# Eighteen feed-forward blocks formed by seven products in place of eight

## The chip, the cores and the metric

The kernel runs on one core of a Trainium2 chip. The metric is the time of one execution on the device, in microseconds (us); the kernel before takes 2004.53 us, the median of three runs (2004.17 to 2005.12). Five engines run their own queues of instructions side by side: PE (TensorE, the matrix products), DVE (VectorE), ACT (ScalarE), POOL (GpSimd) and SP (SyncE, which here only issues transfers). They exchange data through the on-chip memory SBUF and the accumulator banks PSUM, and wait for each other by semaphores.

## The reference, cut to what matters

The program is a stack of two blocks: first two layers of mixers at width 1024, then a block with a mixer and a feed-forward part. The change concerns the feed-forward part, whose mathematics is

```
def conv_gated_mlp(xn, w_up_gate, conv_w_ffn, w_down):
    u, g = jnp.split(xn @ w_up_gate, 2, axis=-1)
    u = causal_dwconv_2(u, conv_w_ffn)          # three taps over the positions
    return (jax.nn.gelu(u) * g) @ w_down

ffn = conv_gated_mlp(rms_norm(h, g_pre_ffn), w_up_gate, conv_w_ffn, w_down)
h = h + rms_norm(ffn, g_post_ffn)
```

with 512 tokens behind 16 meta tokens, D = 1024, 2 x 2816 columns of `w_up_gate`, all float32. The kernel forms 516 of the 528 positions here: four meta tokens are enough for the taps.

## The kernel before

Activations lie transposed, channels on the 128 partitions and positions along the free axis, as eight tiles for the 1024 channels (the K tiles). A float32 value is carried as the sum of a high and a low part in a format that PE multiplies at full rate, so one float32 product is three PE products: high by high, low by high, high by low (`mm3`, lines L101 to L103 of the trace). A `split` makes the parts: a cast on ACT gives the high part (L77), a subtraction on DVE gives the low part (L78); `split_scaled` (L81 and L82) does the same with the gain of the norm multiplied in.

The feed-forward loop runs over 22 pairs: pair m forms block m of u and block m of g, each 128 columns of `w_up_gate`. For a block, SP loads its weights into `wraw` (128 x 8 x 128, 512 KB, three buffers), ACT and DVE split them into `whi` and `wlo` (128 x 1024, three buffers), and PE forms two halves of 258 positions (the g block leaves out the meta tokens: 254 and 258), each 8 K tiles x 3 products. A pair is so 96 products on PE. The norm's factor per position, `rb` (tile `rbc` in the trace), is not in the activations yet: DVE multiplies it in as it empties the PSUM bank (L1274 into `u`, L1284 into `act`). Then come the taps (a tensor_scalar at L1276 and two scalar_tensor_tensor at L1278, all DVE, 128 x 512), the gelu on ACT (L1280) and the gate, `act * cv`, on POOL (L1285). Pairs 6 to 13 also turn one eighth of the residual `h` round by four PE transposes (L1263) and four DVE copies (L1265). After the 22 pairs the products with `w_down` (`ps_d`) follow, for which `act` is split too, into `xh` and `xl`.

The order of instructions on every engine is set by a scheduler that plans the program with a model of its times; the code gives the order of the data only. Every engine takes its instructions in that fixed order, and an instruction that waits holds up all behind it. Tiles come from pools with a fixed number of buffers, and a new tile waits until the buffer's last reader is done. Six PSUM banks (2 to 7) serve the products of this part, and two serve the transposes and the statistics (`ps_st`, L228) of the norm ahead of it.

Of the kernel before, what the change touches and what calls it, by code (L numbers as in the profile page):

```python
# [34 lines left out]
def kernel(ctx: ExitStack, tc: tile.TileContext, a, out):  # L35
# [355 lines left out]
    def tok_proj(w, c0, xs, raw=None):  # L391
        """256 columns, tokens on partitions: yields (t, psum)."""
# [9 lines left out]
    def tok_pairs(w, c0, xs, fine):  # L402
        """The same with the products of two t in one bank."""
# [12 lines left out]
    # ======================= layer 0 =======================  # L416
    w = a["l0_w_in"]
    with ExitStack() as l0:
# [7 lines left out]
        # what the end of a part uses, on the other side: the next part begins before it is free  # L426
# [13 lines left out]
        def silu_gate(ps):  # L440
            """silu of a z projection"""
# [14 lines left out]
        m_st = lt("m_st", n=(4, 128), dt=BF16)  # [s, t]: -NEG where s > t, for each chunk  # L456
# [6 lines left out]
        # input gates from row 0 on, forget gates from row 32 on  # L463
# [27 lines left out]
        V.tensor_tensor(ig, ig, em, op=ALU.subtract)  # a = i - b  # L491
# [25 lines left out]
        # values by token, a column of ones behind them  # L517
# [22 lines left out]
        def others():  # L540
            """The other parameters, the meta tokens, lambda."""
# [21 lines left out]
            # -(e1 - e2 + lam_init)  # L563
# [11 lines left out]
        for hd_ in range(4):  # L575
# [13 lines left out]
            # scores, keys on partitions  # L589
# [8 lines left out]
            # keys by token, weighted  # L598
# [6 lines left out]
            # states before chunks 1 to 3: [C | n], and the output of every chunk: [numerator | denominator]  # L605
# [28 lines left out]
            # output gate, norm, z gate  # L634
# [37 lines left out]
        for hd_ in range(8):  # L672
            j = hd_ % 2
            # queries [high 0, low 0], [low 1, high 1]; keys [high 0, high 0], [high 1, high 1], [low 0, low 1]
# [14 lines left out]
            # [low 1, low 1], so that products into one bank for both maps use all rows  # L689
# [7 lines left out]
            # the maps transposed, blocks [key block, query block] for key blocks up to the query block  # L697
# [6 lines left out]
            for qb in range(4):  # L704
# [4 lines left out]
                # both maps in one bank where they fit  # L709
# [23 lines left out]
                # e0/l0 - lam e1/l1  # L733
# [49 lines left out]
    # ======================= layer 1 =======================  # L783
# [4 lines left out]
    with ExitStack() as l1:  # L788
# [6 lines left out]
        with tc.tile_pool(name="l1", bufs=1) as lp:  # L795
# [12 lines left out]
            triu = lt("triu", 1, 128)  # 1 where column >= partition  # L808
# [17 lines left out]
                # the high and the low part side by side: products of 256 columns  # L826
# [57 lines left out]
    # ======================= block two: mixer =======================  # L884
    w = a["w_in_2"][0]
    with ExitStack() as b2:
# [23 lines left out]
        # the meta tokens at rows 0 and 32 of every product for their keys (for the two heads of a pair), and again  # L910
        # 64 rows on, where the lower part of their values goes
# [20 lines left out]
        # minus one where the key in the row is not before the key in the column  # L932
# [4 lines left out]
        m_st = mt_("m_st", 1, (2, 128), BF16)  # [s, q], twice: NEG where s >= q  # L937
        m_qm = mt_("m_qm", 1, (2, 4), BF16, MR)  # the same, queries from Q0
# [26 lines left out]
        # values by token: [head 0 | zeros | head 1] for each pair of heads and key block  # L965
# [3 lines left out]
        # keys 2 of the second head above zeros, so that both heads' products into one bank use all rows  # L969
# [4 lines left out]
        def values(g):  # L974
            """Two pairs of heads."""
# [32 lines left out]
        def soft(ps, p=128, n=S):  # L1008
            """log(1 + e^z), as float32 and split; z clamped above, where the factor left is zero in float32."""
# [36 lines left out]
        for m in range(KT):  # L1046
            kt = tt("t1", 2)
            evac_r(proj2(next(kw_), xs, 0, 264), 0, 264, kt)
            # keys [high 0, low 0], [low 1, high 1]; queries twice [high 0, high 0], [high 1, high 1]
# [62 lines left out]
            for hh in range(2):  # L1112
                # keys 1 and 3, then keys 0
# [137 lines left out]
    with ExitStack() as ff:  # L1251
# [6 lines left out]
        def residual(i):  # L1258
# [5 lines left out]
            for t in range(4):  # L1264
                V.tensor_copy(ht[t][:, i * 128:(i + 1) * 128], ps[:, t * 128:(t + 1) * 128])  # L1265
# [87 lines left out]
```

## Time and profile before

| | before |
|---|---|
| median of three runs | 2004.53 us |
| profiled execution, its span | 2002.4 us |
| busy: PE | 1980.3 us (99%) |
| busy: DVE | 1261.7 us (63%) |
| busy: ACT | 964.3 us (48%) |
| busy: POOL | 252.0 us (13%) |
| the feed-forward pairs 0 to 21, about | 1633 to 1883 us |
| the down projection, about | 1883 to 1996 us |

The profile comes from one execution; its span, from the first to the last instruction, is 2.1 us under the median of the runs. The busy time of an engine is the time in which at least one of its instructions ran. PE's products are pipelined, so that one that is shown to take 0.28 us may start 0.12 us behind the one before; what a product costs is therefore read from the time of a stretch over its count, not from its own duration. A row of the timeline gives start, duration, engine, line, operation, what was written from what, the tile's size, how many such instructions are drawn together, and in square brackets how long the engine sat idle ahead of it and what ended that. `L78` is line 78 of the kernel before.

### The profile page before, as it was taken

How to read it: one execution, taken by the hardware profiler on the slowest of the kernel's cores; microseconds unless marked ns; L12 is line 12 of the kernel's file. 1: busy time of each engine (PE TensorE's matmuls, PEld its weight loads, DVE VectorE, ACT ScalarE, POOL GpSimd, SP SyncE). 2: the span in 40 equal slices, each digit the busy share in tenths (PEclk: the TensorE clock that was granted, in tenths of full speed). 3: DMA queues.
4: the chain of work that ended last, by engine and by line, in shares of the span. 5: the costliest groups of instructions: out<-in, count | busy, mean ns of one | idle time of the engine just before them, and what ended most of it. 6: DMA issues, size and time to landing. Idle time of an engine off the chain costs nothing.

```text
span 2002.4 us, 33293 instructions
## 1 busy us (share of the span) xinstructions
PE 1980.3 (99%) x13398; PEld 1805.0 (90%) x13398; DVE 1261.7 (63%) x2143; ACT 964.3 (48%) x1815; POOL 252.0 (13%) x339
## 2 busy tenths in 40 slices
PE   8999999999999999999999999999999999999998
PEld 6999988887899888889999999999999999999886
DVE  6667667668662576664877867677344485565533
ACT  5555566668655643354745544545222452222322
POOL 1011000000030111100521212110001031111000
PEclk9999999999999999999999999999999999999999
DMA  6223332222433333243221222222333533333332
GB/s 175 70 75 88 85 85 65 73 74 75 142 115 105 88 97 87 85 138 117 86 64 44 64 61 61 60 64 64 101 95 95 154 111 101 111 91 95 95 95 74
DMA packets 259768, 181.36 MB, mean 91 GB/s; under 512 B 8866, under 2 KB 244607, under 8 KB 259615
## 3 DMA queue, kind: packets, MB, share of 16 engines
q1 hardware_dynamic: 258303, 178.69, 30.0%
q8 instruction: 105, 1.72, 0.4%
q0 software_dynamic: 256, 0.52, 0.1%
q14 instruction: 48, 0.39, 0.1%
q10 hardware_dynamic: 1056, 0.04, 0.0%
HBM read 168.59 MB, written 10.63 MB: 90 GB/s over the span
## 4 chain that ended last, share of the span: by engine, by line
PE 95%; DVE 3%; ACT 1%; DMA 1%; issue 0%; POOL 0%; DVEq 0%; POOLq 0%; ACTq 0%
PE ps L101 18%; PE ps L103 17%; PE ps L102 17%; PE ps_v L103 5%; PE ps_v L101 5%; PE ps_v L102 5%; PE ps_o L101 3%; PE ps_o L102 3%; PE ps_o L103 3%; PE ps_d L101 2%; PE ps_d L103 2%; PE ps_d L102 2%; PE ps_z L1028 2%; PE ps_o L1108 1%; DVE yo L266 1%; PE ps_z L1081 1%
## 5 line engine op out<-in xcount | busy, mean ns | idle before, releaser
L102 PE MATMUL ps<-xl,whi 128*128 128x258 f32 (+3 forms) x2112 | 654.5, 311 | 3.1 <-DVE xl L82 3.0
L101 PE MATMUL ps<-xh,whi 128*128 128x258 f32 (+3 forms) x2112 | 654.7, 313 | 0.8 <-ACT xh L81 0.6
L103 PE MATMUL ps<-xh,wlo 128*128 128x258 f32 (+3 forms) x2112 | 653.7, 311 | 0.0
L77 ACT CAST whi<-wraw 128x1024 fp32r<-128x1024 f32 (+2 forms) x315 | 314.6, 1004 | 471.5 <-PE ps L102 284.8
L78 DVE TENSOR_TENSOR wlo<-wraw,whi 128x1024 fp32r<-128x1024 f32 (+2 forms) x315 | 390.2, 1243 | 180.6 <-ACT whi L77 178.2
L102 PEld LDWEIGHTS ps<-xl,whi 128*128 128x128 f32 x2112 | 399.1, 189 | 27.9 <-DVE xl L82 4.7
L103 PEld LDWEIGHTS ps<-xh,wlo 128*128 128x128 f32 x2112 | 398.5, 189 | 24.2 <-issue 0.5
L101 PEld LDWEIGHTS ps<-xh,whi 128*128 128x128 f32 x2112 | 396.8, 189 | 25.6 <-ACT xh L81 1.5
L101 PE MATMUL ps_v<-whi,xh 128*128 128x256 f32 x896 | 254.2, 285 | 4.5 <-ACT xh L81 4.1
L103 PE MATMUL ps_v<-whi,xl 128*128 128x256 f32 x896 | 253.4, 285 | 1.4 <-DVE xl L82 1.3
L102 PE MATMUL ps_v<-wlo,xh 128*128 128x256 f32 x896 | 254.2, 285 | 0.0
L101 PEld LDWEIGHTS ps_v<-whi,xh 128*128 128x128 f32 x896 | 169.4, 189 | 7.4 <-ACT xh L81 5.6
L103 PEld LDWEIGHTS ps_v<-whi,xl 128*128 128x128 f32 x896 | 169.8, 190 | 3.2 <-DVE xl L82 2.4
L102 PEld LDWEIGHTS ps_v<-wlo,xh 128*128 128x128 f32 x896 | 170.3, 190 | 1.5 <-issue 0.2
L103 PE MATMUL ps<-hi,wlo 128*128 128x258 f32 x384 | 108.6, 283 | 0.0
L101 PE MATMUL ps<-hi,whi 128*128 128x258 f32 x384 | 107.7, 282 | 0.0
L895 DVE TENSOR_TENSOR t<-ps,rbc 128x258 f32<-128x258 f32 (+1 forms) x96 | 40.3, 424 | 64.1 <-PE ps L103 63.5
L102 PE MATMUL ps_o<-xl,whi 128*128 128x512 f32 x192 | 75.6, 394 | 0.0
L101 PE MATMUL ps_o<-xh,whi 128*128 128x512 f32 x192 | 75.4, 395 | 0.0
L103 PE MATMUL ps_o<-xh,wlo 128*128 128x512 f32 x192 | 74.5, 394 | 0.0
L103 PEld LDWEIGHTS ps<-hi,wlo 128*128 128x128 f32 x384 | 72.6, 189 | 0.0
L101 PEld LDWEIGHTS ps<-hi,whi 128*128 128x128 f32 x384 | 72.4, 189 | 0.0
(536 smaller groups left out, 3443.6 us busy)
## 6 DMA issues: line engine op xcount, KB each, us to landing
wraw<-in_l_w_in_dram SPq DMA_DIRECT2D x112, 512.0 KB
wraw<-in_w_in_dram SPq DMA_DIRECT2D x64, 512.0 KB
wraw<-in_w_up_gate_dram SPq DMA_DIRECT2D x44, 512.0 KB
wraw<-in_l_w_out_dram SPq DMA_DIRECT2D x24, 512.0 KB
wraw<-in_w_down_dram SPq DMA_DIRECT2D x22, 512.0 KB
wraw<-in_l_w_out_dram SPq DMA_DIRECT2D x16, 256.0 KB
wraw<-in_w_proj_attn_dram SPq DMA_DIRECT2D x8, 512.0 KB
wraw<-in_w_proj_conv_dram SPq DMA_DIRECT2D x8, 512.0 KB
```

The lines of the kernel that those rows point to most:

```text
L77: A.copy(hi, src)
L78: V.tensor_tensor(lo, src, hi.bitcast(F32), op=ALU.subtract)
L101: T.matmul(ps, lhsT=ah, rhs=bh, start=first, stop=False, **kw)
L102: T.matmul(ps, lhsT=ah, rhs=bl, start=False, stop=False, **kw)
L103: T.matmul(ps, lhsT=al, rhs=bh, start=False, stop=last, **kw)
L266: mult = (G if i % 4 == 3 else V).tensor_tensor(yo[i][:, c], yo[i][:, c], r[:, c], op=ALU.mult)
L895: V.tensor_tensor(dst[:, i * hn:(i + 1) * hn], ps, rb[:, c0 + i * hn:c0 + (i + 1) * hn], op=ALU.mult)
L1028: T.matmul(ps, lhsT=m_, rhs=x_[:, c0:c0 + n], start=False, stop=False, **kw)
L1081: T.matmul(ps, lhsT=k2[hh][r, ks], rhs=ql[r, qs], start=False, stop=False, **kw)
L1108: T.matmul(po[:, n0:], lhsT=l_[:, b, hh:hh + 2, :].rearrange("p a d -> p (a d)"), rhs=a_[r_][:, c0:c0 + S - n0], start=po_first[0], stop=F ...
```

## The change

The sum over K is cut into its two halves (K tiles 0 to 3 and 4 to 7), the positions into their two halves of 258, and the pair of blocks u and g is taken together: u and g, at both halves of the positions, are the four blocks of a product of two 2 x 2 block matrices. Such a product needs eight block products in the plain way. Strassen's identity, in the form of Winograd, needs seven, with sums and differences of blocks ahead of them and behind them. The change uses it for pairs 4 to 21; pairs 0 to 3 stay as they were.

- **Weights.** `seven_w` forms four sums of 128 x 512 on POOL, in the tiles `sa` and `sb`, and splits 3.5 tiles of 128 x 1024 (`r1`, `sa`, `sb`, half of `r2`) in place of two.
- **Activations.** The identity adds positions of one half to those of the other, so the norm's factor has to be in the activations first. Beside pairs 0 to 3, `xn` is formed from `h`, the gain and `rb` (DVE, 128 x 516, eight times), then `seven_x` forms four differences of 128 x 258 on POOL for each of four couples of K tiles, and splits 258, 516 and 1032 columns of each.
- **Products.** Seven products of 4 K tiles x 3 x 258 columns make 84 instructions on PE per pair. ACT copies four results from PSUM to SBUF (`keep`, tile `sn`), DVE adds a PSUM bank and such a copy three times (`o11`, `o12`, `o21`, in place of the four multiplications by `rb`), POOL adds two copies once (`o22`).
- **Around it.** `h` gets a pool of its own, `ht` and `hl` use buffers of the pool `xs`, the last gain is loaded after the pairs. The eight spatial weights of layer 1 are loaded by SP's queue, no longer by POOL's.

```diff
@@ helpers beside mm3 and proj @@
+    HK = KT // 2
+
+    def add(o, x_, y_, op=ALU.add, eng=None):
+        return (eng or G).tensor_tensor(o, x_, y_, op=op)
+
+    def seven_w(pool, r1, r2):
+        sa = pool.tile([128, KT, 128], F32, tag="sa", name="sa", bufs=4)
+        sb = pool.tile([128, KT, 128], F32, tag="sa", name="sb", bufs=4)
+        lo, hi = slice(0, HK), slice(HK, KT)
+        add(sb[:, lo], r2[:, lo], r2[:, hi])
+        add(sa[:, lo], sb[:, lo], r1[:, lo], ALU.subtract)
+        add(sa[:, hi], r1[:, lo], r2[:, lo], ALU.subtract)
+        add(sb[:, hi], r1[:, hi], sa[:, lo], ALU.subtract)
+        w = {}
+        for raw, names in ((r1, "12"), (sa, "67"), (sb, "53"), (r2[:, hi], "4")):
+            sp_ = split_w(raw)
+            ...
+        return w
+
+    def seven_x(pool, tmp, p, xa, xb, n, out):
+        tq = tmp.tile([128, 4, n], F32, tag="tq", name="tq")
+        h0, h1 = slice(0, n), slice(n, 2 * n)
+        t1, t2, t3, t4 = (tq[:, i] for i in range(4))
+        add(t1, xa[:, h1], xa[:, h0], ALU.subtract)
+        add(t3, xb[:, h1], xa[:, h1], ALU.subtract)
+        add(t2, xb[:, h1], t1, ALU.subtract)
+        add(t4, xb[:, h0], t2, ALU.subtract)
+        for src, names in ((xa[:, h0], "1"), (xb, "23"), (tq.rearrange("p a b -> p (a b)"), "5674")):
+            sp_ = [pool.tile([128, n * len(names)], F32R, tag=f"sx{names}{r}{p}", name=f"sx{r}") for r in "hl"]
+            split(src, *sp_)
+            ...
+
+    def seven(sw, sx, n, snp, o11, o12, o21, o22):
+        def product(nm, b, start):
+            if start:
+                bank[b] = pst("mm", n, f"ps_s{b}")
+            wh, wl = sw[nm]
+            for k in range(HK):
+                mm3(bank[b], wh[:, k], wl[:, k], *sx[nm, k], start and k == 0, k == HK - 1, **kw)
+            return bank[b]
+
+        def keep(ps):
+            t_ = snp.tile([128, n], F32, tag="sn", name="sn", bufs=5)
+            A.copy(t_, ps)
+            return t_
+
+        s1 = keep(product("1", "x", True))
+        add(o11, product("2", "y", True), s1, eng=V)
+        u2 = keep(product("6", "x", False))
+        s7 = keep(product("7", "w", True))
+        u4 = keep(product("5", "x", False))
+        add(o12, product("3", "z", True), u4, eng=V)
+        add(o22, u4[:, n - n22:], s7[:, n - n22:])
+        add(o21, product("4", "w", False)[:, n - n21:], u2[:, n - n21:], eng=V)
@@ layer 1, spatial weights @@
-                G.dma_start(wsr, a["l1_w_spatial"][g])
+                nc.sync.dma_start(wsr, a["l1_w_spatial"][g])
@@ feed-forward, residual(i) @@
-            hl = fp.tile([128, S], F32, tag="hl", name="hl")
+            if i % 4 == 0:
+                for t in range(4):
+                    ht[t][i // 4] = xsp.tile([128, S], F32, tag="xs", name="ht")
+            hl = xsp.tile([128, S], F32, tag="xs", name="hl")
@@ feed-forward, pairs @@
-        for m in range(22):
-            wt = next(uw)
+        FIRST = 4
+        for m in range(FIRST):
+            wt = split_w(load_w(wu, 0, KT, m * 128, 128))
             u = fp.tile([128, NQ], F32, tag="u", name="u")
             for i in range(2):
                 ps = proj(wt, xs, i * HQ, HQ)
                 V.tensor_tensor(u[:, i * HQ:(i + 1) * HQ], ps, rb[:, i * HQ:(i + 1) * HQ], op=ALU.mult)
             ...
             G.tensor_tensor(act[m], act[m], cv, op=ALU.mult)
+            xn = []
+            for i in (m, m + HK):
+                xn.append(ft.tile([128, NQ], F32, tag="xn", name="xn", bufs=2))
+                V.scalar_tensor_tensor(xn[-1], h[i], pv("g_pre_ffn_2", i), rb[:, :NQ], op0=ALU.mult, op1=ALU.mult)
+            seven_x(fx, ft, m, *xn, HQ, sx)
+        for m in range(FIRST, 22):
+            u = fp.tile([128, NQ], F32, tag="u", name="u")
+            sw = seven_w(fw, *(load_w(wu, 0, KT, c + m * 128, 128) for c in (0, FF)))
+            seven(sw, sx, HQ, fw, u[:, :HQ], u[:, HQ:], act[m][:, :HQ - 4], act[m][:, HQ - 4:])
+            cv = conv_gelu(m, u)
+            G.tensor_tensor(act[m], act[m], cv, op=ALU.mult)
             if 6 <= m < 14:
                 residual(m - 6)
```

The taps and the gelu (`conv_gelu`) are what they were. In the rows that follow, the names are those of the program, a number behind a name tells its buffers apart, and L126 is the line of `add`, L78 the split, L173 the `keep`.

POOL in the steady part of the pairs, before, where five rows are five pairs:

```order
L1285 TENSOR_TENSOR act_17813<-act_17813,cv 128x512
L1285 TENSOR_TENSOR act_17814<-act_17814,cv 128x512
L1285 TENSOR_TENSOR act_17815<-act_17815,cv 128x512
L1285 TENSOR_TENSOR act_17816<-act_17816,cv 128x512
L1285 TENSOR_TENSOR act_17817<-act_17817,cv 128x512
```

Each is the gate of one pair, and nothing else stands on POOL in this part.

The same place after, from the gate of pair 7 to that of pair 8:

```order
L1377 TENSOR_TENSOR act7_17818<-act7_17818,cv_18967 128x512
L126 TENSOR_TENSOR act8_17819<-sn_19081,sn_19067 128x258
L126 TENSOR_TENSOR sb_19278<-wraw_19275 128x512
L126 TENSOR_TENSOR sa_19277<-wraw_19273,wraw_19275 128x512
L126 TENSOR_TENSOR sa_19277<-sb_19278,wraw_19273 128x512
L126 TENSOR_TENSOR sb_19278<-wraw_19273,sa_19277 128x512
L1377 TENSOR_TENSOR act8_17819<-act8_17819,cv_19111 128x512
```

Between two gates there was nothing on POOL; now `o22` of pair 8 stands there, and the four sums of the weights of pair 10.

DVE in the steady part, before: one pair, from the low part of one block's weights on:

```order
L78 TENSOR_TENSOR wlo<-wraw,whi 128x1024
L1274 TENSOR_TENSOR u<-ps,rbc 128x258 x2
L1276 TENSOR_SCALAR cv<-u,pcol 128x512
L78 TENSOR_TENSOR wlo<-wraw,whi 128x1024
L1278 SCALAR_TENSOR_TENSOR cv<-u,pcol,cv 128x512
L1284 TENSOR_TENSOR act_17821<-ps,rbc 128x254
L1278 SCALAR_TENSOR_TENSOR cv<-u,pcol,cv 128x512
L1284 TENSOR_TENSOR act_17821<-ps,rbc 128x258
```

Two splits of weights, and four reads of PSUM with `rb`, stand in each pair. The same engine after, one pair: the low parts of pair 9's weights, between them the work on pair 9's results:

```order
L78 TENSOR_TENSOR wlo_19284<-wraw_19273,whi_19283 128x1024
L78 TENSOR_TENSOR wlo_19288<-sa_19277,whi_19287 128x1024
L126 TENSOR_TENSOR u_19128<-ps_sz_19227,sn_19225 128x258
L126 TENSOR_TENSOR act9_17820<-ps_sw_19198,sn_19196 128x254
L78 TENSOR_TENSOR wlo_19292<-sb_19278,whi_19291 128x1024
L1340 TENSOR_SCALAR cv_19255<-u_19128,pcol_84 128x512
L126 TENSOR_TENSOR u_19272<-ps_sy_19314,sn_19312 128x258
L78 TENSOR_TENSOR wlo_19296<-wraw_19275,whi_19295 128x512
L1342 SCALAR_TENSOR_TENSOR cv_19255<-u_19128,pcol_84,cv_19255 128x512 x2
```

Two splits of a pair have become three and a half, and the four reads of PSUM three.

DVE at the passage from the plain pairs to pair 4, after: the end of what is formed beside pairs 0 to 3, and the low parts that pair 4 needs of its sums (`sa`, `sb`); `ht` is the residual by token, `xl` from `act` a split for the down projection.

```order
L1342 SCALAR_TENSOR_TENSOR cv<-u,pcol,cv 128x512
L1334 COPY ht<-ps_h 128x128 x8
L78 TENSOR_TENSOR sxl<-tq,sxh 128x1032
L1334 COPY ht<-ps_h 128x128 x8
L126 TENSOR_TENSOR u<-ps_sy,sn 128x258
L78 TENSOR_TENSOR xl<-act_17811,xh 128x512
L78 TENSOR_TENSOR xl<-act_17812,xh 128x512
L1334 COPY ht<-ps_h 128x128 x4
L78 TENSOR_TENSOR xl<-act_17813,xh 128x512
L1334 COPY ht<-ps_h 128x128 x4
L78 TENSOR_TENSOR xl<-act_17814,xh 128x512
L78 TENSOR_TENSOR wlo<-sa,whi 128x1024
```

The residual's copies, one group of four beside each of eight pairs before, now stand at this place, 28 of the 32 ahead of `wlo` of `sa`, and with them four splits for the down projection. In the plain pairs before, the rows at this place are those of the steady part.

## Rows read from the trace of the kernel before

**Rows 1.** The page: busy us of each engine, share of the span, instructions.

```profile
PE 1980.3 (99%) x13398; PEld 1805.0 (90%) x13398; DVE 1261.7 (63%) x2143; ACT 964.3 (48%) x1815; POOL 252.0 (13%) x339
```

**Rows 2.** The page: chain that ended last, shares of the span by engine.

```profile
PE 95%; DVE 3%; ACT 1%; DMA 1%; issue 0%; POOL 0%; DVEq 0%; POOLq 0%; ACTq 0%
```

**Rows 3.** Waits of PE, longest first: total us, times, longest us.

```profile
PE ps_x L374 <- POOL acc L465: 4.7, 1, 4.7
```

**Rows 4.** Windows: us; busy PE, PEld, DVE, ACT, POOL; clock; DMA share, GB/s.

```profile
1805.33:1816.81 11.48, 11.48 (x98) 11.48 (x98) 6.25 (x9) 3.01 (x4) 1.30 (x1) 1.00 0.32 93
1746.12:1758.05 11.93, 11.93 (x102) 11.93 (x101) 7.18 (x14) 2.73 (x4) 1.31 (x1) 1.00 0.38 111
1637.00:1883.00 246.00, 246.00 (x2023) 244.23 (x2021) 150.31 (x236) 66.11 (x77) 29.18 (x22) 1.00 0.35 103
1883.00:1996.00 113.00, 112.66 (x488) 91.22 (x486) 39.32 (x46) 31.52 (x51) 0.00 (x0) 1.00 0.27 88
```

**Rows 5.** Groups, 1400 to 2003 us: count, busy us, mean ns, idle before.

```profile
L78 DVE TENSOR_TENSOR xl<-act,xh 128x512 fp32r<-128x512 f32 x22 | 15.5, 721 | 40.4 <-ACT xh L77 40.4
L1265 DVE COPY ht<-ps_h 128x128 f32<-128x128 f32 x32 | 7.0, 282 | 0.1
L77 ACT CAST whi<-wraw 128x1024 fp32r<-128x1024 f32 x99 | 103.7, 1050 | 249.1 <-PE ps L102 176.7 <-issue 57.4 <-DMA wraw<-in_w_down_dram 6.6
L1280 ACT ACTIVATE cv<-cv 128x512 f32<-128x512 f32 x22 | 13.9, 632 | 59.0 <-DVE cv L1278 58.9
L256 ACT ACTIVATE yo<-ps,pcol 128x258 f32<-128x258 f32 x16 | 7.6, 475 | 13.8 <-PE ps L103 13.8
```

**Rows 6.** Timeline, DVE in a late pair: start, duration, instruction.

```profile
1845.49 0.49 DVE L1276 TENSOR_SCALAR cv<-u,pcol 128x512 f32<-128x512 f32 x1
1845.96 1.23 DVE L78 TENSOR_TENSOR wlo<-wraw,whi 128x1024 fp32r<-128x1024 f32 x1
1847.10 0.75 DVE L1278 SCALAR_TENSOR_TENSOR cv<-u,pcol,cv 128x512 f32<-128x512 f32 x1
1847.79 0.42 DVE L1284 TENSOR_TENSOR act<-ps,rbc 128x254 f32<-128x254 f32 x1
```

**Rows 7.** Timeline, the same pair: the gate on POOL and a split on DVE.

```profile
1839.77 1.30 POOL L1285 TENSOR_TENSOR act<-act,cv 128x512 f32<-128x512 f32 x1 [10.18 <-DVE act L1284]
...
1840.21 1.94 DVE L78 TENSOR_TENSOR wlo<-wraw,whi 128x1024 fp32r<-128x1024 f32 x1 [0.58 <-ACT whi L77]
```

**Rows 8.** Timelines of DVE and POOL, an early pair: the split came first.

```profile
1653.44 1.23 DVE L78 TENSOR_TENSOR wlo<-wraw,whi 128x1024 fp32r<-128x1024 f32 x1
...
1654.01 1.82 POOL L1285 TENSOR_TENSOR act<-act,cv 128x512 f32<-128x512 f32 x1 [6.49 <-ACT cv L1280]
```

**Rows 9.** Timelines of DVE and POOL in the norm ahead, 258 columns each.

```profile
1612.71 0.42 DVE L207 TENSOR_TENSOR acc<-acc,sq 128x258 f32<-128x258 f32 x1
...
1613.39 0.97 DVE L82 SCALAR_TENSOR_TENSOR xl<-yc,pcol,xh 128x258 fp32r<-128x258 f32 x1
1614.28 0.97 DVE L266 TENSOR_TENSOR yo<-yo,rbc 128x258 f32<-128x258 f32 x1
1615.17 0.97 DVE L82 SCALAR_TENSOR_TENSOR xl<-yc,pcol,xh 128x258 fp32r<-128x258 f32 x1
...
1612.33 3.52 POOL L207 TENSOR_TENSOR acc<-acc,sq 128x258 f32<-128x258 f32 x3 [1.75 <-ACT sq L206]
...
1622.21 0.74 POOL L207 TENSOR_TENSOR acc<-acc,sq 128x258 f32<-128x258 f32 x1 [1.99 <-ACT sq L206]
```

**Rows 10.** Timelines: last sums of the norm on PE, its factor on ACT.

```profile
1633.79 0.60 PE L228 MATMUL ps_st<-acc,ones 128*128 128x258 f32 x2
...
1637.03 0.42 ACT L219 ACTIVATE rbc<-rbc 128x258 f32<-128x258 f32 x1
```

**Rows 11.** Windows about a gap of PE, columns as in rows 4.

```profile
1617.20:1620.50 3.30, 1.43 (x10) 1.24 (x11) 3.27 (x6) 1.48 (x4) 2.22 (x3) 1.00 0.24 80
1620.60:1623.90 3.30, 3.09 (x15) 2.79 (x14) 3.30 (x8) 2.29 (x6) 1.39 (x2) 0.50 0.36 120
1624.00:1627.30 3.30, 3.30 (x28) 3.24 (x27) 3.06 (x7) 2.37 (x6) 1.60 (x3) 1.00 0.24 80
```

**Rows 12.** Transfers: issuing queue, count, KB each, us to landing.

```profile
wsr<-in_l_w_spatial_dram POOLq DMA_DIRECT2D x8, 64.0 KB, 2.2
```

More of the change, by code (lines that the diff above doesn't have):

```diff
@@ L98, in split_w @@
         return hi, lo
+    kw = dict(skip_group_check=True)
     def mm3(ps, ah, al, bh, bl, first, last, **kw):
@@ L117, in proj @@
         return ps
+    HK = KT // 2
[12 more added lines that the diff above has]
+            sp_ = split_w(raw)
+            for i, nm in enumerate(names):
+                w[nm] = [x_[:, i * HK:(i + 1) * HK] for x_ in sp_]
+        return w
@@ new lines, in seven_x @@
+    def seven_x(pool, tmp, p, xa, xb, n, out):
[9 more added lines that the diff above has]
+            split(src, *sp_)
+            for i, nm in enumerate(names):
+                out[nm, p] = [x_[:, i * n:(i + 1) * n] for x_ in sp_]
@@ new lines, in seven @@
+    def seven(sw, sx, n, snp, o11, o12, o21, o22):
+        bank = {}
+        def product(nm, b, start):
[15 more added lines that the diff above has]
+        add(o12, product("3", "z", True), u4, eng=V)
+        n22, n21 = o22.shape[1], o21.shape[1]
+        add(o22, u4[:, n - n22:], s7[:, n - n22:])
+        add(o21, product("4", "w", False)[:, n - n21:], u2[:, n - n21:], eng=V)
@@ L1219 @@
         yo = [mx.tile([128, NQ], F32, tag=f"part{i}", name=f"yo{i}") for i in range(KT)]
-        h[:] = [ring("yc") for i in range(KT)]
+        hr = tc.alloc_tile_pool(name="hr", bufs=1, side="right", reuse_waits="tile")
+        h[:] = [hr.tile([128, NQ], F32, tag=f"h{i}", name=f"h{i}") for i in range(KT)]
         for i in range(KT):
@@ L1251 @@
     with ExitStack() as ff:
-        fp = ff.enter_context(tc.tile_pool(name="fp", bufs=2))
+        fp = ff.enter_context(tc.tile_pool(name="fp", bufs=2, reuse_waits="tile"))
         act = [fp.tile([128, S], F32, tag=f"act{i}", name=f"act{i}", bufs=1) for i in range(22)]
-        gpb = fp.tile([128, D], F32, tag="gpb", name="gpb", bufs=1)
-        ht = [fp.tile([128, D], F32, tag=f"ht{t}", name=f"ht{t}", bufs=1) for t in range(4)]
+        ht = [[None, None] for t in range(4)]
         def residual(i):
-            hl = fp.tile([128, S], F32, tag="hl", name="hl")
+            if i % 4 == 0:
+                for t in range(4):
+                    ht[t][i // 4] = xsp.tile([128, S], F32, tag="xs", name="ht")
+            hl = xsp.tile([128, S], F32, tag="xs", name="hl")
             nc.sync.dma_start(hl, hd[i][:, META:])
@@ L1264, in residual, with conv_gelu @@
             for t in range(4):
-                V.tensor_copy(ht[t][:, i * 128:(i + 1) * 128], ps[:, t * 128:(t + 1) * 128])
+                V.tensor_copy(ht[t][i // 4][:, i % 4 * 128:(i % 4 + 1) * 128], ps[:, t * 128:(t + 1) * 128])
         wu = a["w_up_gate_2"][0]
-        uw, gw = w_cols(wu, 0, FF), w_cols(wu, FF, FF, 1)
-        for m in range(22):
-            wt = next(uw)
-            u = fp.tile([128, NQ], F32, tag="u", name="u")
-            for i in range(2):
-                ps = proj(wt, xs, i * HQ, HQ)
-                V.tensor_tensor(u[:, i * HQ:(i + 1) * HQ], ps, rb[:, i * HQ:(i + 1) * HQ], op=ALU.mult)
+        def conv_gelu(m, u):
             cv = fp.tile([128, S], F32, tag="cv", name="cv")
@@ L1280 @@
             last["gelu"] = A.activation(cv, cv, AF.Gelu_apprx_tanh)
-            wt = next(gw)
+            return cv
+        FIRST = 4
+        fx = tc.alloc_tile_pool(name="fx", bufs=1, reuse_waits="tile")
+        ft = tc.alloc_tile_pool(name="ft", bufs=1, side="right", reuse_waits="tile")
+        sx = {}
+        for m in range(FIRST):
+            wt = split_w(load_w(wu, 0, KT, m * 128, 128))
+            u = fp.tile([128, NQ], F32, tag="u", name="u")
+            for i in range(2):
+                ps = proj(wt, xs, i * HQ, HQ)
+                V.tensor_tensor(u[:, i * HQ:(i + 1) * HQ], ps, rb[:, i * HQ:(i + 1) * HQ], op=ALU.mult)
+            cv = conv_gelu(m, u)
+            wt = split_w(load_w(wu, 0, KT, FF + m * 128, 128), parts=1 if m else 4)
             for c0, c1 in ((4, HQ), (HQ, NQ)):
@@ L1302 @@
             raw = load_w(wd, k, 1, 0, 1024)
-            wh, wl = (x_[:, 0, :] for x_ in (split_w(raw) if k < 18 else split_w(raw, fp, f"l{k % 2}")))
+            wh, wl = (x_[:, 0, :] for x_ in (split_w(raw) if k < 18 else split_w(raw, fd, f"l{k % 2}")))
             ah, al = (x_[:, :S] for x_ in new_xs())
```

21 lines of the change are left out of this document (14 added, 7 removed).

## The prediction

> **What bounds the kernel now.** First the page's busy times: PE runs 1980.3 us of the span of 2002.4 us, DVE under two thirds of it, POOL an eighth [rows 1]. The chain that ended last is PE for 95% [rows 2], and the longest wait of PE in the whole run is 4.7 us, at the start of the program, far from the changed part [rows 3]. Then the windows of the changed part. A plain pair late in the loop takes 11.48 us, all of them PE; one that carries a piece of the residual 11.93 us, for its four transposes; the whole stretch of the pairs has no gap on PE, with DVE at 150 of 246 us and POOL at 29 [rows 4]. So a product fewer on PE is worth its full time, as long as nobody else takes longer than PE. The down projection behind it is PE's as well. Each pair's 96 products share its 11.48 us, 0.1196 us for one.
>
> Next, what the two engines that get more work cost each other. The gate on POOL takes 1.30 us by itself. A split of 1024 columns on DVE takes 1.23 us; the one that started 0.44 us into a gate took 1.94 us [rows 6, 7]. It ended at 1842.15; had it been held until the gate was nearly over and then run its own 1.23 us, it started in effect at 1840.92, 1.15 us into the gate. The other way round, a gate that started 0.57 us into a split took 1.82 us [rows 8], 0.52 longer, and the split had 0.66 left. In the norm ahead of the loop, where both have work without a break, DVE's 258 columns take 0.97 us where they take 0.42 alone, one DVE step starts every 0.89 us, and POOL's three take 3.52 us, where one alone takes 0.74 [rows 9]. **The two take turns:** while one has two operands in SBUF, the other, reading SBUF, stands still, but for about the last 0.15 us. DVE's steps in a row also start 0.08 us before the end of the one ahead (1.23 after 1845.96 is 1847.19, and the next started at 1847.10) [rows 6].
>
> **PE.** Pairs 4 to 21 have 84 products, all of 258 columns: 84 x 0.12 = 10.1 us, 1.4 us less than 11.48, 25 us over 18 pairs. That is the whole gain there can be.
>
> **DVE and POOL in a steady pair.** POOL had one gate; now it has four sums of 512 columns, `o22` of 258 and the gate. The sums have the gate's shape, so POOL holds the turn 5 x (1.30 - 0.15) + (0.74 - 0.15) = 6.3 us [rows 6, 7, 9]. DVE has three splits of 1024, one of 512 (0.72 with waits in it [rows 5], 0.69 taken), a tensor_scalar of 0.49 and two steps of 0.75 [rows 6], each less 0.08: 3.45 + 0.61 + 0.41 + 1.34 = 5.8 us in which it needs the turn. The three reads of PSUM (0.42 us each) need one SBUF operand only and are taken to run beside POOL. Together 12.1 us, more than PE's 10.1 us and 0.6 us more than the pair took. The price is bounded below by no taking of turns at all: then DVE needs 5.8 + 1.0, POOL 7.2, and PE's 10.1 us is the pair. It is bounded above by whole durations, 7.24 + 6.36 = 13.6 us. I take 12.1, since it uses what the three overlaps measured.
>
> One rule speaks of this place. The Trainium skill (SBUF — State Buffer, Who interferes with whom) says that a DVE instruction with two SBUF inputs contends with a GpSimd instruction that reads SBUF, and that whoever issues first holds the shared ports while the other fully blocks. The trace agrees on who blocks whom, but the split of 1.94 us shows a block that ends 0.15 us before the gate does [rows 7]; by the rule's letter the sum would be the 13.6 us above.
>
> **ACT and the loads.** ACT has 3.5 casts of 1.05, a gelu of 0.63 and four reads of PSUM of 0.48 at most [rows 5], 6.2 us of 12: hidden behind PE and DVE. The loads keep their count; the DMA share was 0.32 to 0.38 [rows 4]. The same work of the residual is elsewhere, so its transposes cost what they did. The eight spatial weights on SP's queue each wait for a transpose of the group two before, and layer 1's loads stand behind them; the transposes are long past by then, so I take nothing. If that cover is gone, a load is late by about the 2.2 us that such a transfer takes [rows 12], up to 15 us for seven.
>
> **The passage to pair 4.** Behind the last sums of the norm (1633.8 us) PE has, up to the first product with `wlo` of `sa`, ten halves of 24 products, 24 of pair 4, six high parts and the 32 transposes (0.45 / 4 = 0.11 us each [rows 4]): 270 x 0.1196 + 3.6 = 35.9 us, so it gets there at about 1670. The norm's factor is there at 1637.5 [rows 10]. From then on, up to that `wlo`, DVE needs the turn for four splits of 1024 (4.6), eight normed tiles of 516 (5.4, as the steps of 0.75), the splits of x (1.4 + 2.4 + 4.6), four tensor_scalars and eight steps of the taps (1.6 + 5.4) and four splits of `act` (2.4): 27.8 us. POOL has 16 differences (16 x 0.59 = 9.4), four gates and four sums (8 x 1.15 = 9.2): 18.6 us. In turns 46.4 us, to 1684. PE waits 14 us there; with about 3 us, an estimate, for places where both wait for someone's operands, 17 us. Lower bound, by DVE alone: 27.8, 28 copies of 0.22 (7.0 us for 32 [rows 5]) and 14 reads of PSUM of 0.34, 38.8 us, so PE waits 7. Upper bound, by whole durations: 24.
>
> **The sum.** From pair 4 on 17 intervals at 12.1 in place of 11.48 are +10.5; the eighteenth keeps PE's gain, -1.4; the passage is +17. So 2002.4 + 26.1 = 2028.5 us of span, and 2.1 us more for the median of the runs over the span: about 2030 us.
>
> **Rivals.** *Faster: POOL's work hides.* If the sums and `o22` run beside DVE, PE stays the bound: 18 x -1.4 + 7 at the passage, 1987 us. It decides from the point where a pair falls under 10.9 us (17 x 0.6 = 10 us of gain against a passage of some 12). For it: DVE would be busy 6.8 of 10.1 us and POOL 7.2, neither full; the splits run a pair ahead, so one late split holds nobody at first. Against it: all three overlaps in the rows held the second instruction, and nearly all that is added is of the same shapes. 0.14.
>
> *About even.* Part of the turns falls under PSUM reads or under steps that do not hold, and a pair takes some 10.9 us: 2004. 0.06.
>
> *Whole blocks.* If the second waits out the first entirely, 17 x 2.1 - 1.4 + 24 + 2.1 gives 2063 us, by the upper bounds. Against it stand the measured 1.94 and 1.82 us. 0.07.
>
> *The clock falls as well.* After a stretch in which PE was busy 1.43 of 3.30 us, the next had the granted clock at 0.50, which is 1.2 in place of 2.4 GHz, and then 1.00 again [rows 11]. Here PE would wait 2 us in each pair of 12. Were each pair to have one such slow stretch, it would lose 1.65 us of PE work; PE then needs 11.8 us of the 12.1, so little or all of it may show: up to 17 x 1.65 = 28 us, 2058. Against it: PE is busy 84% of a pair. 0.10.
>
> **How the numbers follow.** The turns with the sizes above have 0.63; with the two cases beyond it, slower has 0.80. Faster has 0.14, within 0.2% (4 us, about what a measurement of this kernel can tell from no change) 0.06. Within the likeliest case a pair of 11.5 to 12.6 us and a passage of 8 to 24 us give 2008 to 2046; the range goes on to 2060 to take in the clock's case and most of the whole blocks. The faster rival lies outside it.
>
> **What would show it.** In the changed kernel's windows a pair of 18 at 12.1 us, PE busy about 10 of them, clock 1.00; PE's waits led by `wlo` (L78), and the chain passing from PE to DVE and POOL in this part; splits of 1024 on DVE with means near 1.9 to 2.2 us in place of 1.23, POOL's 512 columns well above 1.30 in the mean, and hardly a moment with neither at work. At the passage one wait of PE of 10 to 20 us on `wlo` of `sa`. If PE has no gaps and a pair takes 10.1 us, the taking of turns is wrong as a price. If pairs are at 12.1 but the splits have their old 1.23 us, something else holds them: loads, or buffers of `wraw` and `sa` that come free late.

## The result and the profile after

The changed kernel takes 2026.92 us (median of four runs, 2026.19 to 2026.96), the kernel before, run beside it, 2004.35 us: a ratio of 1.0111, with a 95% interval of 1.0097 to 1.0126. It is 22.6 us slower, with 216 matrix products less. The prediction was about 2030 us.

The page after gives the busy time of each engine, and who holds the chain that ended last:

```profile
PE 1972.7 (97%) x13182; PEld 1788.7 (88%) x13182; DVE 1364.5 (67%) x2181; ACT 1019.7 (50%) x1935; POOL 418.1 (21%) x437
...
PE 85%; DVE 10%; issue 2%; ACT 2%; POOL 1%; DMA 1%; DVEq 0%; ACTq 0%; POOLq 0%
```

Against [rows 1, 2], PE is busy 8 us less and the span is 23 us longer, 2025.3 us. (The 216 products are worth more, about 26 us at 0.12 us; the part on the clock below says where some of it went.) The chain has gone from 95% PE to 85%, and most of what PE lost went to DVE. PE's waits in the changed part, where before there was none to speak of, are these (total us, times, longest us):

```profile
PE ps_sx L105 <- DVE wlo L78: 20.7, 15, 2.2
PE ps_h L1332 <- DVE ht L1334: 7.2, 4, 2.8
PE ps_sy L104 <- DVE sxl L78: 1.7, 1, 1.7
```

The first row is one wait in nearly every pair, for the low part of the next pair's weights; the second and the third are the passage to pair 4. The windows, with the columns of [rows 4], show two pairs and the passage:

```profile
1754.03:1765.74 11.71, 10.44 (x84) 10.18 (x84) 11.17 (x11) 5.27 (x10) 9.39 (x6) 1.00 0.31 90
1765.74:1777.44 11.70, 10.44 (x84) 10.18 (x84) 11.17 (x11) 5.28 (x10) 9.35 (x6) 1.00 0.31 92
1637.00:1685.90 48.90, 39.03 (x293) 36.76 (x291) 48.90 (x85) 20.13 (x29) 29.03 (x24) 0.88 0.34 102
```

A pair has 84 products and takes 11.7 us. DVE, which was busy 6.25 of 11.48 us, is busy 11.17; POOL 9.4 where it was 1.3. What DVE is busy with is seen in the timeline of the first of the two pairs, first a part of DVE's steps, then POOL's:

```profile
1756.58 0.41 DVE L126 TENSOR_TENSOR u<-ps_sz,sn 128x258 f32<-128x258 f32 x1
1756.92 0.41 DVE L126 TENSOR_TENSOR act<-ps_sw,sn 128x254 f32<-128x254 f32 x1
1757.25 1.21 DVE L78 TENSOR_TENSOR wlo<-sb,whi 128x1024 fp32r<-128x1024 f32 x1
1758.38 1.51 DVE L1340 TENSOR_SCALAR cv<-u,pcol 128x512 f32<-128x512 f32 x1
1759.82 0.41 DVE L126 TENSOR_TENSOR u<-ps_sy,sn 128x258 f32<-128x258 f32 x1
1760.15 1.45 DVE L78 TENSOR_TENSOR wlo<-wraw,whi 128x512 fp32r<-128x512 f32 x1
1761.52 3.48 DVE L1342 SCALAR_TENSOR_TENSOR cv<-u,pcol,cv 128x512 f32<-128x512 f32 x2
...
1758.22 1.40 POOL L126 TENSOR_TENSOR sb<-wraw 128x512 f32<-128x512 f32 x1 [0.95 <-DMA wraw<-in_w_up_gate_dram]
1759.57 1.48 POOL L126 TENSOR_TENSOR sa<-wraw 128x512 f32<-128x512 f32 x1
1761.00 1.74 POOL L126 TENSOR_TENSOR sa<-sb,wraw 128x512 f32<-128x512 f32 x1
1762.82 1.63 POOL L126 TENSOR_TENSOR sb<-wraw,sa 128x512 f32<-128x512 f32 x1
```

While POOL had nothing, a split of 1024 took its 1.21 us. From 1758.22 on the two step through each other: the tensor_scalar takes 1.51 in place of 0.49, the split of 512 1.45 in place of some 0.69, the two taps 3.48 in place of 1.5, and POOL's sums up to 1.74 in place of 1.30. Most of DVE's busy time beyond 6.8 us is standing still. The reads of PSUM keep their 0.41 us.

### The profile page after: what moved, and what is told of

Same layout as the page of the kernel before. It is cut to its first block, busy times and chain, and to the rows that moved or that the text cites. A ratio compares the mean times of both kernels' runs of the same rounds, so it can differ in the third digit from the quotient of the medians.

```text
span 2025.3 us, 33104 instructions
## 1 busy us (share of the span) xinstructions
PE 1972.7 (97%) x13182; PEld 1788.7 (88%) x13182; DVE 1364.5 (67%) x2181; ACT 1019.7 (50%) x1935; POOL 418.1 (21%) x437
## 3 DMA queue, kind: packets, MB, share of 16 engines
q8 instruction: 103, 1.69, 0.3%
## 4 chain that ended last, share of the span: by engine, by line
PE 85%; DVE 10%; issue 2%; ACT 2%; POOL 1%; DMA 1%; DVEq 0%; ACTq 0%; POOLq 0%
PE ps L103 13%; PE ps L105 13%; PE ps L104 13%; PE ps_v L103 5%; PE ps_v L105 5%; PE ps_v L104 5%; PE ps_o L103 3%; PE ps_o L104 3%; PE ps_o L105 3%; DVE wlo L78 2%; PE ps_d L103 2%; PE ps_d L105 2%; PE ps_d L104 2%; PE ps_z L1094 2%; PE ps_o L1174 1%
## 5 line engine op out<-in xcount | busy, mean ns | idle before, releaser
L77 ACT CAST whi<-wraw 128x1024 fp32r<-128x1024 f32 (+2 forms) x315 | 306.9, 979 | 407.8 <-PE ps L104 169.9
L78 DVE TENSOR_TENSOR wlo<-wraw,whi 128x1024 fp32r<-128x1024 f32 (+2 forms) x315 | 389.8, 1243 | 172.5 <-ACT whi L77 170.6
L104 PE MATMUL ps<-xl,whi 128*128 128x258 f32 (+3 forms) x1536 | 492.4, 322 | 3.8 <-DVE xl L82 3.8
L103 PE MATMUL ps<-xh,whi 128*128 128x258 f32 (+3 forms) x1536 | 491.7, 324 | 1.1 <-ACT whi L77 0.4
L105 PE MATMUL ps<-xh,wlo 128*128 128x258 f32 (+3 forms) x1536 | 491.1, 321 | 0.0
L104 PEld LDWEIGHTS ps<-xl,whi 128*128 128x128 f32 x1536 | 290.3, 189 | 28.9 <-DVE xl L82 5.8
L103 PEld LDWEIGHTS ps<-xh,whi 128*128 128x128 f32 x1536 | 288.2, 189 | 26.3 <-issue 1.2
L105 PEld LDWEIGHTS ps<-xh,wlo 128*128 128x128 f32 x1536 | 289.7, 189 | 24.0 <-issue 0.5
L105 PE MATMUL ps_sx<-sxh,wlo 128*128 128x258 f32 x216 | 63.8, 295 | 20.8 <-DVE wlo L78 20.7
```

The costliest lines, as they stand in the source:

```text
L103: T.matmul(ps, lhsT=ah, rhs=bh, start=first, stop=False, **kw)
L104: T.matmul(ps, lhsT=ah, rhs=bl, start=False, stop=False, **kw)
L105: T.matmul(ps, lhsT=al, rhs=bh, start=False, stop=last, **kw)
```

## Which theory: four kernels about the pairs and the passage

Theory: DVE and POOL take turns at SBUF (when both read it, one of them stands still), and the sum of their turns sets the pair. Rivals: the splits, casts or loads hold the pair and the sums are hidden; DVE is simply full; the loss lies evenly in the pairs.

**The sums taken away** (`no_sums`). In `seven_w` the four sums go, and the raw weights are split in their place, so that the products are no longer those of the identity:

```diff
-        add(sb[:, lo], r2[:, lo], r2[:, hi])
-        add(sa[:, lo], sb[:, lo], r1[:, lo], ALU.subtract)
-        add(sa[:, hi], r1[:, lo], r2[:, lo], ALU.subtract)
-        add(sb[:, hi], r1[:, hi], sa[:, lo], ALU.subtract)
-        for raw, names in ((r1, "12"), (sa, "67"), (sb, "53"), (r2[:, hi], "4")):
+        for raw, names in ((r1, "12"), (r2, "67"), (r1, "53"), (r2[:, hi], "4")):
```

> Left out: the four sums of weights on POOL in each of the 18 pairs; the raw weights are split and multiplied in their place, so the splits, casts, products and reads are as many as in the changed kernel and only POOL's sums are gone. Theory (DVE and POOL take turns): in a pair POOL needs the turn for 1.74 us in place of 6.3, DVE 5.8, together 7.5 us, under PE's 10.1; PE bounds the pair again, 17 x (10.1 - 11.76) = -28 us and about 5 us less at the passage: 1994 us (1988 to 2000). Rival (the splits, casts or loads bound the pair, the sums are hidden beside them): within 5 us of the changed kernel's 2027.

Measured: 1989.28 us, 0.9927 of the kernel before (0.9911 to 0.9944). In the windows of two pairs PE has no gap, and DVE does the same eleven steps in 7.0 us:

```profile
1755.10:1765.30 10.20, 10.20 (x86) 10.15 (x86) 7.01 (x11) 5.50 (x9) 2.80 (x2) 1.00 0.38 110
1765.30:1775.50 10.20, 10.20 (x86) 10.15 (x85) 7.01 (x11) 5.50 (x9) 2.80 (x3) 1.00 0.34 98
```

So four sums on POOL, another engine, are what makes DVE's eleven steps 11.17 us long. Casts, splits and loads are all still there and hold nobody.

**The sums on DVE** (`sums_dve`). Each of the four is given `eng=V`:

```diff
-        add(sb[:, lo], r2[:, lo], r2[:, hi])
+        add(sb[:, lo], r2[:, lo], r2[:, hi], eng=V)
...
```

> The four sums of weights of each pair are formed on DVE in place of POOL. Theory (turns): a sum of 512 columns holds the turn 0.61 us on DVE and 1.15 on POOL, so the work in turns falls from 12.1 to 5.8 + 2.4 + 1.7 = 10.0 us, about PE's 10.1; a pair takes 10.2 to 10.8 in place of 11.76, the whole 2001 to 2011 us, below the changed kernel by 16 to 26. Rival (DVE, busy 11.2 of 11.7 us of a pair, is simply full, and POOL is not): 2.4 us more work on the full engine, 17 x 2.4 = 41 us longer than the changed kernel, 2068.

Measured: 2000.12 us, 0.9982 of the kernel before (0.9973 to 0.9991): 27 us under the changed kernel, 1 us under the range that the theory gave, and 0.2% under the kernel before as well. Windows of two pairs, and the groups of one stretch of ten pairs:

```profile
1755.82:1766.07 10.25, 10.25 (x86) 10.16 (x85) 10.25 (x15) 5.36 (x10) 3.77 (x3) 1.00 0.37 107
1766.07:1776.30 10.23, 10.23 (x86) 10.18 (x85) 10.23 (x15) 5.39 (x10) 3.77 (x3) 1.00 0.35 100
```

```profile
L78 DVE TENSOR_TENSOR wlo<-sa,whi 128x1024 fp32r<-128x1024 f32 x10 | 23.3, 2328 | 0.0
L1342 DVE SCALAR_TENSOR_TENSOR cv<-u,pcol,cv 128x512 f32<-128x512 f32 x19 | 14.1, 741 | 0.0
L78 DVE TENSOR_TENSOR wlo<-sb,whi 128x1024 fp32r<-128x1024 f32 x10 | 12.1, 1208 | 0.0
...
L126 DVE TENSOR_TENSOR sa<-sb,wraw 128x512 f32<-128x512 f32 x10 | 6.8, 680 | 0.0
```

More work was given to the engine that was busy 95% of the pair, and the pair went from 11.7 to 10.24 us. A sum takes 0.68 us on DVE against 1.30 on POOL, and it takes no turn away from anybody. The taps are back at 0.74 us; one split of 1024 still pays, with 2.33 us, for the gate that is left on POOL. That DVE was "full" is refuted: its busy time held POOL's turns.

**One sum more on POOL** (`sum_extra`), into a tile that nobody reads:

```diff
         add(sb[:, lo], r2[:, lo], r2[:, hi])
+        add(pool.tile([128, HK, 128], F32, tag="se", name="se", bufs=1), r1[:, lo], r2[:, hi])
```

> One more sum of 512 columns on POOL in each of the 18 pairs, into a tile that nobody reads. Theory (turns): 1.15 us more per pair, 17 x 1.15 = 20 us and 1 at the passage, 2047 us (2042 to 2052). Rival (POOL has 2.3 us to spare in each pair of 11.7 and its work is hidden): within 4 us of the changed kernel's 2027.

Measured: 2047.26 us, 20.3 us over the changed kernel. POOL had 2.3 us of idle time in each pair, and yet one sum more costs 1.13 us per pair (20.3 over 18), about the 1.15 that was taken for one turn. The gates of pairs 8 to 18 lie 13.0 us apart in the mean, where they lie 11.9 apart in the changed kernel.

**Eight plain pairs ahead** (`first8`). The pieces of the residual move along, to pairs 8 to 15.

```diff
-        FIRST = 4
+        FIRST = 8
...
+            if m < HK:
...
-            if 6 <= m < 14:
-                residual(m - 6)
+            if 8 <= m < 16:
+                residual(m - 8)
```

> Eight plain pairs ahead in place of four, so 14 pairs of seven products in place of 18; the normed x and its differences are still formed beside the first four, the residual beside pairs 8 to 15. Theory (the passage cost some 16 us because 46 us of work in turns stood against 36 us of PE): with four more plain pairs PE has 82 us of work and the passage costs at most 3; 13 intervals at 11.76 against 11.48 add 4 us, the last pairs give back 3 to 4: 2004 to 2009 us, although four pairs fewer use the identity. Rival (the loss lies evenly in the pairs of seven products): 14 of 18 of the loss of 22.6 stays, 2022 us.

Measured: 2007.73 us, 1.0020 of the kernel before (1.0010 to 1.0029). PE has no wait over 2.2 us left, while the pairs of seven still take 11.7 us. Four pairs fewer with the identity, and 19 us less: the passage was a cost by itself, paid once. That PE had too little to do beside it is the theory's reading, and the time fits it; the residual's copies moved in the same edit, and this run doesn't separate the two. (`sums_first6` below leaves the residual at pairs 6 to 13, and there too two plain pairs more take PE's waits on the copies away.)

## Where the passage goes, and a version under both kernels

The sums on DVE leave 18 to 19 us at the passage: 17 intervals at 10.24 in place of 11.48 and one at -1.4 would give about 1982. PE's waits there led with 7.4 us on the residual's copies, behind which its transposes stand in order. Four kernels start from `sums_dve`: `copies_act` has the first edit below, `sums_first6` the second, `best6` both, and `best5` both with `FIRST = 5`.

```diff
-                V.tensor_copy(ht[t][i // 4][:, i % 4 * 128:(i % 4 + 1) * 128], ps[:, t * 128:(t + 1) * 128])
+                A.copy(ht[t][i // 4][:, i % 4 * 128:(i % 4 + 1) * 128], ps[:, t * 128:(t + 1) * 128])
...
-        FIRST = 4
+        FIRST = 6
```

> As sums_dve (sums of weights on DVE), and the residual's 32 copies out of PSUM made by ACT. Theory (at the passage DVE's queue is what PE waits for, copies included, and PE's transposes stand in order behind the copies): 28 copies of 0.2 us leave DVE ahead of the first split of a sum, 6 us, and PE's waits on them, 7.4 us, shrink; 6 to 9 us under sums_dve: 1991 to 1995. Rival (the copies fill time in which POOL holds the turn and cost nothing): 1998 to 2002, as sums_dve.

Measured: 1997.05 us, 3.1 us less, half of what was expected. The wait went on to ACT: PE's two longest waits here are

```profile
PE ps_sx L103 <- ACT whi L77: 3.9, 1, 3.9
PE ps_h L1332 <- ACT ht L1334: 2.1, 1, 2.1
```

since ACT makes the high parts of `x` and of the weights behind the copies. `wlo` of `sa` starts at 1681.85, 3.2 us earlier than in `sums_dve` (1685.10).

> As sums_dve, with six plain pairs ahead in place of four (16 pairs of seven products); the normed x is formed beside the first four. Theory (of the 18 to 19 us that the passage costs, what two plain pairs' 23 us of PE work less their 11 us of DVE work cover goes, 12 us, and two pairs at 11.48 in place of 10.24 cost 2.5): 1989 to 1993 us. Rival (the passage is a wait in the pairs themselves, such as first loads or first sums, and moves along): 2002 to 2004.

Measured: 1996.16 us, 3 to 7 us above the expectation. PE's waits on the copies are gone, but six small ones of up to 1.8 us on `wlo` follow it, 5.0 us in all, between 1706 and 1794 us. A likely reason, which no run tests by itself: with the sums, DVE's pair of 10.24 us is no shorter than PE's 10.2, so what DVE brings along from the passage is not worked off.

> Both: sums of weights on DVE, copies on ACT, six plain pairs ahead. Theory: the passage costs 0 to 4 us, 16 pairs at 10.24 in place of 11.48 gain 20: 1984 to 1988 us. Rival (one of the two edits already takes all that the passage has to give): 1990 to 1994, as the better of the two.

Measured: 1992.96 us, above the expectation by 5; PE's waits in the part add up to 7 us where 0 to 4 were expected. The time lies in the rival's range, but 3.2 us under the better of the two single edits, so neither edit takes all that the passage has to give.

> As best6 with five plain pairs ahead. One pair more of seven products gains 1.2 us; the passage has 11.5 us of PE work less 5.4 of DVE work to hide behind, 6 us less cover than with six. Theory: 1984 to 1991 us, at or above best6 if the passage still shows, 1.2 below it if it doesn't.

Measured: **1988.85 us, 0.9925 of the kernel before (0.9910 to 0.9940)**, with the reference's whole computation, and as fast as the kernel that leaves the sums out. It lies 4.1 us under `best6`: 1.2 us for the pair, and 2.9 us fewer of PE's waits (3.8 us in all in place of 6.7). The order that the scheduler makes differs from kernel to kernel; why this one has fewer waits was not tested.

**The first tap on ACT.** The tensor_scalar, one operand in SBUF, was held like the others above. It was moved, in the changed kernel (`tap_act`) and in `best5` (`best5_tap`):

```diff
-            V.tensor_scalar(cv, u[:, 4:], pv("conv_w_ffn_2", 44 + m), None, op0=ALU.mult)
+            A.activation(cv, u[:, 4:], AF.Copy, scale=pv("conv_w_ffn_2", 44 + m))
```

> The changed kernel with one edit: the first tap's multiplication (tensor_scalar, 128 x 512, one operand in SBUF) is made by ACT in all 22 pairs. Theory (this step takes its turn against POOL like those of two operands: in the steady pairs its mean is 1.1 us against 0.49 alone): 0.35 us of turns less in each pair, 17 x 0.35 = 6 us and 1 at the passage, 2020 us (2018 to 2023). Rival (a step of one operand takes no turn and merely stood behind others): 2025 to 2027, no difference. Second rival (the pair is a circle through ACT, since PE waits for low parts that wait for ACT's casts behind the gelu): 0.6 us more on that circle, 2030 or over.

Measured: 2053.19 us (five of six runs 2051.3 to 2054.4, one 2033.9), 26 us above the changed kernel. The theory and its first rival are both wrong on it; the second rival's "2030 or over" has the sign. PE's longest group of waits, and ACT in one pair:

```profile
PE ps_sx L103 <- ACT sn L173: 36.4, 15, 4.0
```

```profile
1784.12 0.63 ACT L1344 ACTIVATE cv<-cv 128x512 f32<-128x512 f32 x1 [2.38 <-DVE cv L1342]
1784.66 0.36 ACT L173 COPY sn<-ps_sx 128x258 f32<-128x258 f32 x1
1784.91 0.38 ACT L173 COPY sn<-ps_sw 128x258 f32<-128x258 f32 x1
1787.91 1.05 ACT L77 CAST whi<-sa 128x1024 fp32r<-128x1024 f32 x1 [2.62 <-PE ps_sx L104]
```

The scheduler put the copies of two products behind the gelu. ACT stands 2.38 us waiting for the taps, the copies wait behind that, and PE cannot begin the next product in that bank; then the cast waits for PE. In the changed kernel the two copies stand ahead of the gelu. From gate to gate the pairs take 13.0 and 14.2 us, most of them in turns, and the longer ones go with a lower granted clock:

```profile
1771.82:1784.83 13.01, 10.48 (x84) 10.18 (x84) 10.39 (x10) 6.22 (x11) 9.85 (x7) 1.00 0.30 83
1784.83:1798.99 14.16, 11.81 (x84) 11.51 (x84) 10.39 (x10) 6.21 (x11) 9.85 (x7) 0.88 0.26 75
```

So of the 26 us a part is the new order and a part, 1.15 us in each longer pair, the clock. What set the one run of 2033.9 apart stays open: only one of the others was profiled. The size of the tap's turn can't be read from this run; it shows what a moved instruction can do through the order.

> best5 with the same edit. With the sums on DVE a pair takes 10.24 us where PE's products need 10.18, and DVE has no time to spare to work off what the passage left. Theory: DVE's 0.35 to 0.4 us less per pair bring the pairs to 10.18 (1 us) and shorten the waits behind the passage (1 to 2 us): 1986 to 1988. Rival (PE already bounds all but the passage): as best5, 1988.9, within 0.7 us.

Measured: 1992.26 us, 3.4 us above `best5` (on another chip, where the kernel before took 0.5 us longer): a miss on both the theory and the rival. The pairs take 10.22 us, 10.25 before the edit, so DVE's relief is worth next to nothing where PE bounds the pair, and DVE now waits 23.0 us for ACT's casts over the pairs. Around the passage PE waits 1.1 us more than in `best5`, and behind two of the waits it works without a gap at a lower clock:

```profile
1683.50:1686.80 3.30, 3.30 (x23) 3.30 (x23) 3.30 (x5) 0.39 (x2) 0.61 (x1) 0.72 0.67 248
1700.00:1703.30 3.30, 3.30 (x20) 3.30 (x20) 3.30 (x6) 3.08 (x10) 0.00 (x0) 0.64 0.10 28
```

PE's working time in the pairs, weighed by how far the granted clock lies under 1.00, gives an estimate of 3.2 us lost to the clock, against 1.5 in `best5`. Waits and clock together, 1.1 and 1.7 us, are most of the 3.4.

## Why the prediction was right

**PE and its gain.** 84 products were counted at 10.1 us; with nobody in the way a pair takes 10.2 (no_sums). Right.

**The pair.** Forecast 12.1 us; from the gate of pair 5 (1718.77) to that of pair 19 (1883.40) 14 intervals take 11.76 on average. The mechanism holds: taking turns was shown by taking the sums away (10.2), by adding one (+1.13 per pair) and by moving them (10.24). Whole blocks, 13.6 us, did not come. The size was 0.35 us too large, and the term is DVE's holds: I let a step hold its turn until 0.08 us before its end, how far its own engine's next step overlaps. [rows 8] gave it for POOL: a gate that took 1.82 us and 1.30 alone had in effect started at 1654.53, 0.14 us before the split ended. With 0.14 for DVE's seven steps their turns are 5.4 us, and with POOL's 6.3 the pair is 11.7. The timeline above bears it out: POOL's third sum, 1.74 us from 1761.00 and 1.30 alone, had in effect started at 1761.44, 0.16 us before the split of 512 ended. The rows were there, and were read for one direction alone.

**The passage.** Forecast 17 us, with `wlo` of `sa` at 1684. Its row starts at 1684.67, the product that needs it at 1685.94, 51.9 us behind the last sums of the norm at 1634.08, of which the 270 products and 32 transposes need 35.9: 16.0 us. The sum is right, and DVE, which is busy 48.90 of 48.90 us in its window, is what PE waits for. The picture of one long wait on `wlo` of `sa` is not: PE stands 9.9 us in six waits of 1.0 to 2.8 us, 7.2 of them ahead of the residual's transposes, behind DVE's copies, and only 1.0 on that `wlo`. The other 6 us lie in PE's instructions themselves, which stand further apart there than the count has them, in part at a lower clock.

**The total, and some luck.** Of the 22.6 us of loss the passage is the larger part; the other 6.6, for which 9.1 were forecast, hide two errors against each other. Seventeen intervals at 11.76 are 4.8 us in place of 10.5, and with the last pair's -1.4 only 3.4 would be left. The clock, which the sum had at nothing, makes up the difference.

**The clock.** It was a rival with 0.10, and part of it did come. Windows of 3.3 us through the passage, and at the end of the pairs:

```profile
1670.30:1673.60 3.30, 0.90 (x4) 0.48 (x4) 3.30 (x6) 0.74 (x1) 2.45 (x3) 1.00 0.00 0
1673.60:1676.90 3.30, 1.97 (x8) 1.49 (x8) 3.30 (x9) 3.28 (x7) 1.28 (x1) 0.55 0.00 0
1676.90:1680.20 3.30, 1.97 (x8) 1.50 (x8) 3.30 (x11) 0.00 (x0) 3.24 (x3) 0.50 0.00 0
...
1686.80:1690.10 3.30, 3.30 (x17) 3.30 (x17) 2.69 (x2) 0.38 (x1) 3.30 (x2) 0.50 0.00 0
1690.10:1693.40 3.30, 3.30 (x26) 3.30 (x25) 1.46 (x1) 1.32 (x2) 3.22 (x3) 0.87 0.53 159
...
1881.50:1884.80 3.30, 1.07 (x9) 0.86 (x9) 3.30 (x3) 2.46 (x4) 3.22 (x3) 1.00 0.10 40
1884.80:1888.10 3.30, 3.30 (x20) 3.30 (x20) 3.30 (x4) 0.70 (x2) 2.55 (x2) 0.61 0.47 159
1888.10:1891.40 3.30, 3.30 (x26) 3.30 (x26) 3.20 (x6) 0.62 (x1) 0.00 (x0) 0.87 0.17 17
```

Behind a stretch in which PE was busy 0.90 of 3.30 us the granted clock went to 0.50, 1.2 in place of 2.4 GHz. While PE waited for DVE, which had no gap, that cost nothing; from 1686.80 on, PE is full at half clock and makes 17 products where 28 fit [rows 11], and then 26: by the two rows 3.3 x 0.5 + 3.3 x 0.13 = 2.1 us. At the end of the pairs it fell once more, with PE full again: 3.3 x 0.39 + 3.3 x 0.13 = 1.7 us. Together 3.8 us, and 16.0 + 4.8 - 1.4 + 3.8 is 23.2, where the spans differ by 22.9. In the steady pairs the clock stayed at 1.00, with PE busy 10.4 of 11.7 us, but for one stretch (0.75 and 0.73, 1812.20 to 1818.80). That rival's 28 us did not come.

**What was to be seen.** Waits on `wlo`, a pair of about 12 us, PE busy about 10 of it, the chain passing to DVE: all there. So were POOL's sums of 512 columns above 1.30 us in the mean (1.37 to 1.72 by kind of input), and no moment with neither DVE nor POOL at work: from the gate of pair 5 to that of pair 19 the timelines have none. One sign did not come, the single wait of 10 to 20 us at the passage. And one was set too narrowly: splits of 1024 with means near 1.9 to 2.2 us. In the changed kernel's pairs, by kind of input, the three splits have

```profile
L78 DVE TENSOR_TENSOR wlo<-sa,whi 128x1024 fp32r<-128x1024 f32 x15 | 28.8, 1920 | 4.3 <-ACT whi L77 4.2
L78 DVE TENSOR_TENSOR wlo<-wraw,whi 128x1024 fp32r<-128x1024 f32 x15 | 25.8, 1720 | 0.0
L78 DVE TENSOR_TENSOR wlo<-sb,whi 128x1024 fp32r<-128x1024 f32 x15 | 20.2, 1345 | 0.0
L1342 DVE SCALAR_TENSOR_TENSOR cv<-u,pcol,cv 128x512 f32<-128x512 f32 x30 | 50.7, 1691 | 0.5
L1340 DVE TENSOR_SCALAR cv<-u,pcol 128x512 f32<-128x512 f32 x15 | 16.6, 1105 | 0.0
```

so that by my own words something else could have been suspected. The taps paid more than the splits did, 1.69 us in place of 0.74. Who pays depends on which steps happen to stand beside POOL's sums; only the sum over all of them was forecast, and only it should have been the sign.

**ACT, loads, spatial weights.** ACT was busy 5.3 us of the pair. POOL waits about 1 us per pair for a load of weights, within time in which DVE works. The spatial weights on SP's queue cost nothing to be seen: the last sums of the norm lie at 1634.08 in place of 1633.79 us.

## What to carry to other kernels

When work goes to two idle-looking engines that take turns at SBUF, as DVE and POOL did here, add up their turns, not their busy times: a pair with DVE at 54% and POOL at 11% did not have room for what was added to both. An engine that is "busy 95%" may be standing still for most of what was added, and giving it the other's work can make it faster; price an elementwise sum on both engines (0.68 against 1.30 us here) before choosing POOL for being idle. And a saving on the bounding engine has to bring the work it needs in advance: the passage cost 16 us once, and one plain pair more, with the sums and the copies moved, made it small.

## What the runs showed of the hardware

The tensor_scalar, with one operand in SBUF, was held by POOL just as the two-operand steps were (1.51 us in place of 0.49, beside a sum that started 0.16 us earlier), while steps with one operand in PSUM and one in SBUF were not (means of 0.41 us in a stretch where POOL is busy 80% of the time). The overlap at the end of a turn is nearly the same in both directions: 0.14 us where a gate waited for a split [rows 8], 0.15 where a split waited for a gate [rows 7], 0.16 where a sum waited for a split (1761.00 above).
